# The end of a SwiGLU block: parts of 3, 4 and 4 pairs, half of the residual joined by DMA, and the last norm's two factors in one instruction

## The chip, the cores and the metric

The kernel runs on one core of a Trainium2 chip. Its five engines run on their own queues, each in order: TensorE (PE, matmuls into PSUM banks), VectorE (DVE), ScalarE (ACT), GpSimd (POOL) and SyncE (SP, which issues most DMAs). The metric is the device time of one execution in microseconds; the median of three runs of the kernel before is 1082.09 us (1082.02 to 1082.15).

## The reference

One layer of an encoder block on x of 512 rows and 1024 columns in float32, with the mixers left out here:

```python
x = x + merged @ w_o[l]
h2 = rmsnorm(x, g_ffn[l])
x = x + (jax.nn.silu(h2 @ w_ff_gate[l]) * (h2 @ w_ff_up[l])) @ w_ff_down[l]
return rmsnorm(x, g_final)

def rmsnorm(x, g):
    y = xf * lax.rsqrt(jnp.mean(xf * xf, axis=-1, keepdims=True) + EPS)
    return y * g
```

The hidden width of the SwiGLU is 2816, which is 11 pairs of 256 columns.

## The kernel before, in words

Every float32 product is made of three matmuls: each operand is split into a high part (a cast on ScalarE, L166) and a low part (a subtraction on VectorE, L167), and high x high, high x low and low x high are summed in a bank.

The SwiGLU's products are computed in a Strassen-like form with seven products in place of eight. The activations enter as a11, a12, s1, s2, s3, a22, s4 (quarters of the matrix and their sums), and the weights as seven forms: b11, b21, t1, t2, t3, t4, b22. The t forms are sums of weight quarters that VectorE adds in place (L239) ahead of the split. Up and gate projections go pair by pair: `pair(q)` (L817) makes products with matmuls of 256 columns (L730) and ends in `gated`, which multiplies the two branches (L752, L753), forms the sums for the next product (L769) and splits them into the activation tiles.

The 11 pairs are cut into parts by `FF_PARTS`: 4, 4 and 3 pairs. After each part comes the product with w_ff_down for the pairs of that part, with matmuls of 512 columns (L870 in `prod_tm`), n pairs giving 6 n matmuls for each of the seven forms. After the first two parts, `down` (L878) adds its results into `ydr`, a copy of x in DRAM, with DMAs from GpSimd that accumulate (L876). `x` was written there earlier, after the mixers.

The last part's product is written out from L912 on, and is the place of the change. Six banks hold the results: `a` (two, rows of the first or second half), `b` (two), `d` (two). a11 goes into `a`; a12 into `b`; s1 into `d`; s2 is added onto `a`; s3 onto that; a22 onto that; s4 onto `d`. So `a` has to be read out after a11, after s2 and after s3, before the next of them may write it. In the kernel before, two loads (L914) bring all of x from `ydr` into the tiles `y[0]` and `y[1]` (left and right 512 columns), and VectorE joins every bank with them: `to_y` (L946) adds, L960 and L964 subtract.

The final norm: `square` (L923) sums the squares of one block of 128 rows and one half on ScalarE and multiplies that half by the gain `gf` on VectorE (L924). `early` (L930) takes the half that is complete first, `store` the other: L936 gives the mean of squares, GpSimd raises it to -0.5 (L938), ScalarE scales the left half (L939), VectorE the right (L940), and two DMAs store them (L942). a22 and s4 are the two last products. Each is computed for one block of rows after the other, and `ev_a` or `ev_d` is called after each block, so the four blocks end one after the other.

Weights come in 128 x 1024 tiles through a pool of ten; the split halves `whi` and `wlo` come from pools of five, so a cast waits until the matmuls of the fifth piece before it are done. `PLAN` lists all weight pieces in order, and `take` prepares two ahead (`AHEAD`). The order of instructions on each engine is set when the kernel is built, by a scheduler that may move instructions past one another; within an engine nothing overtakes at run time.

Of the kernel before, what the change touches and what calls it, by code (L numbers as in the profile page):

```python
# [27 lines left out]
EPS = 1e-6  # L28
# [8 lines left out]
QH = CH // 2  # L37
NQ = NFB // 2

FF_PARTS = ((0, 4), (4, 4), (8, 3))  # L40

WARM = 8

# [5 lines left out]
def plan():  # L49
# [89 lines left out]
def block_kernel(ctx: ExitStack, tc: tile.TileContext, xT, xtok, wpack, wquad, cols, decs, rot, g_ffn, g_final, out):  # L139
    nc = tc.nc  # L140
# [5 lines left out]
    small = ctx.enter_context(tc.tile_pool(name="small", bufs=4))  # L146
# [202 lines left out]
    mhalf = const.tile([P, 8], F32, name="mhalf")  # L349
# [49 lines left out]
    for k in range(8):  # L399
# [16 lines left out]
                            op0=ALU.mult, op1=ALU.add)  # L416
    for j in range(15, 0, -2):
# [3 lines left out]
                                   op0=ALU.mult, op1=ALU.mult)  # L421
# [57 lines left out]
    def do_scores(h, qk):  # L479
        tab = decay(h)  # L480
        p = (bigtile(F32R), bigtile(F32R))
        for mb in range(NB):
            ps = bank()
            for d in range(2):
                sl = slice(mb * P, (mb + 1) * P)
                mm3(ps, (qk[0][:, 2 + d, sl], qk[1][:, 2 + d, sl]), (qk[0][:, d, :], qk[1][:, d, :]),
                    d == 0, d == 1)
            t = t512()
            o = (3 - mb) * P
            nc.vector.scalar_tensor_tensor(out=t, in0=ps, scalar=QK ** -0.5, in1=tab[:, o:o + 512],  # L490
                                           op0=ALU.mult, op1=ALU.mult)
            split(t, p[0][:, mb, :], p[1][:, mb, :])
        return p
# [101 lines left out]
    for h in range(HEADS):  # L595
        p = do_scores(h, qk)
# [47 lines left out]
    y = [bigtile(), bigtile()]  # L644
# [6 lines left out]
    ydr = dram.tile([S, D], F32, name="ydr")  # L651
# [48 lines left out]
    for half in range(2):  # L700
        c = Chunk()
# [15 lines left out]

    part_of = {q: (q0, n) for q0, n in FF_PARTS for q in range(q0, q0 + n)}
    act = {}
# [184 lines left out]
    begin(1, 1)  # L904
    for q0, n in FF_PARTS:
        for q in range(max(q0, 1), q0 + n):
# [10 lines left out]
    acs = [small.tile([P, 6], F32, tag="fin", name="fin") for _ in range(NB)]  # L917

    def square(nb, half):

        yt, ac = y[half][:, nb, :], acs[nb]
        sq = t512()
        nc.scalar.activation(sq, yt, AF.Square, accum_out=ac[:, half:half + 1])  # L923
        nc.vector.tensor_tensor(out=yt, in0=yt, in1=gf[:, half * 512:(half + 1) * 512], op=ALU.mult)  # L924

    def early(nb, half):

        square(nb, half)
        ac = acs[nb]
        nc.vector.tensor_scalar(out=ac[:, 3:4], in0=ac[:, half:half + 1], scalar1=1.0 / D, scalar2=EPS,  # L930
                                op0=ALU.mult, op1=ALU.add)

    def store(nb, half):
        square(nb, half)
        ac = acs[nb]
        nc.vector.scalar_tensor_tensor(out=ac[:, 4:5], in0=ac[:, half:half + 1], scalar=1.0 / D,  # L936
                                       in1=ac[:, 3:4], op0=ALU.mult, op1=ALU.add)
        nc.gpsimd.tensor_tensor(out=ac[:, 5:6], in0=ac[:, 4:5], in1=mhalf[:, 0:1], op=ALU.pow)  # L938
        nc.scalar.activation(y[0][:, nb, :], y[0][:, nb, :], AF.Copy, scale=ac[:, 5:6])  # L939
        nc.vector.tensor_scalar_mul(y[1][:, nb, :], y[1][:, nb, :], ac[:, 5:6])  # L940
        for h in (1, 0):
            nc.sync.dma_start(out[nb * P:(nb + 1) * P, h * 512:(h + 1) * 512], y[h][:, nb, :])  # L942

    def to_y(ps, nb, half):
        yt = y[half][:, nb, :]
        nc.vector.tensor_tensor(out=yt, in0=ps, in1=yt, op=ALU.add)  # L946

    a, b, d = ([bank(), bank()] for _ in range(3))
    prod_tm(n, "a11", a, True)
    for tt in range(2):  # L950
        to_y(a[tt], tt, 0)
    prod_tm(n, "a12", b, True, True)
    for tt in range(2):
        to_y(b[tt], tt, 0)
        early(tt, 0)
    prod_tm(n, "s1", d, True)
    prod_tm(n, "s2", a, False)
    for tt in range(2):
        yt = y[1][:, tt, :]
        nc.vector.tensor_tensor(out=yt, in0=yt, in1=a[tt], op=ALU.subtract)  # L960
    prod_tm(n, "s3", a, False)
    for tt in range(2):
        yt = y[1][:, 2 + tt, :]
        nc.vector.tensor_tensor(out=yt, in0=yt, in1=a[tt], op=ALU.subtract)  # L964
        to_y(d[tt], 2 + tt, 1)
        early(2 + tt, 1)

    def ev_a(tt):
        to_y(a[tt], 2 + tt, 0)
        store(2 + tt, 0)  # L970
# [69 lines left out]
```

## Time and profile before

| what | us |
|---|---|
| median of three runs | 1082.09 |
| the profiled execution | 1081.23 |
| its span, first to last instruction | 1079.4 |
| from the end of the last pair's s4 to the end of the last matmul | 30.12 |
| TensorE busy in it | 28.02 |
| from the last matmul's end to the end of the span | 10.29 |

A row of the timeline gives the start, the duration, the engine, the line in the kernel, the operation and the tiles (written <- read), and in brackets how long the engine was idle before it and who ended that. The rows of grouped instructions give the count, busy time in us and the mean duration in ns, and the idle time ahead. A row of the waits gives who waited for whom, the total, the count and the longest, in us. The profiled TensorE clock was 0.997 of full speed.

### The profile page before, as it was taken

How to read it: one execution, taken by the hardware profiler on the slowest of the kernel's cores; microseconds unless marked ns; L12 is line 12 of the kernel's file. 1: busy time of each engine (PE TensorE's matmuls, PEld its weight loads, DVE VectorE, ACT ScalarE, POOL GpSimd, SP SyncE). 2: the span in 40 equal slices, each digit the busy share in tenths (PEclk: the TensorE clock that was granted, in tenths of full speed). 3: DMA queues.
4: the chain of work that ended last, by engine and by line, in shares of the span. 5: the costliest groups of instructions: out<-in, count | busy, mean ns of one | idle time of the engine just before them, and what ended most of it. 6: DMA issues, size and time to landing. Idle time of an engine off the chain costs nothing. (4 is left out here: it accounts for less than half of the span.)

```text
span 1079.4 us, 13769 instructions
## 1 busy us (share of the span) xinstructions
PE 1062.5 (98%) x5560; PEld 913.8 (85%) x5560; DVE 743.5 (69%) x1012; ACT 429.8 (40%) x569; POOL 34.1 (3%) x50
## 2 busy tenths in 40 slices
PE   8999999999999999999999999999999999999995
PEld 7888888888888888888888888889998899989974
DVE  7846574757575746955364444459898979897997
ACT  7352244225222522222132323345555545554544
POOL 0000000000000000000000000000000100011001
PEclk9999999999999999999999999999999999999998
DMA  7322222212221322042323232922331942256402
GB/s 264 130 95 88 68 94 83 78 59 98 79 78 59 118 82 94 22 135 89 106 97 99 95 101 93 355 98 60 100 115 33 243 118 97 79 158 145 166 1 78
DMA packets 35727, 114.69 MB, mean 106 GB/s; under 512 B 4048, under 2 KB 4048, under 8 KB 35664
## 3 DMA queue, kind: packets, MB, share of 16 engines
q1 hardware_dynamic: 33360, 109.62, 30.4%
q0 software_dynamic: 2304, 4.20, 2.7%
q8 instruction: 43, 0.70, 0.3%
q14 instruction: 20, 0.16, 0.0%
HBM read 105.41 MB, written 8.39 MB: 105 GB/s over the span
## 5 line engine op out<-in xcount | busy, mean ns | idle before, releaser
L166 ACT CAST whi<-raw 128x1024 fp32r<-128x1024 f32 (+1 forms) x236 | 241.1, 1029 | 405.6 <-PE bank L281 136.8
L167 DVE TENSOR_TENSOR wlo<-raw,whi 128x1024 fp32r<-128x1024 f32 (+1 forms) x236 | 280.6, 1196 | 171.4 <-ACT whi L166 170.4
L281 PE MATMUL bank<-big,whi 128*128 128x512 f32 x640 | 249.0, 389 | 0.0
L280 PE MATMUL bank<-big,whi 128*128 128x512 f32 x640 | 249.0, 389 | 0.0
L282 PE MATMUL bank<-big,wlo 128*128 128x512 f32 x640 | 249.0, 389 | 0.0
L730 PE MATMUL bank<-xform,whi 128*128 128x256 f32 x1248 | 227.9, 284 | 1.2 <-ACT t L826 1.2
L730 PEld LDWEIGHTS bank<-xform,whi 128*128 128x128 f32 x1248 | 194.8, 192 | 4.4 <-ACT t L826 2.4
L730 PE MATMUL bank<-xform,wlo 128*128 128x256 f32 x624 | 175.6, 283 | 0.0
L281 PEld LDWEIGHTS bank<-big,whi 128*128 128x128 f32 x640 | 120.1, 188 | 25.0
L280 PEld LDWEIGHTS bank<-big,whi 128*128 128x128 f32 x640 | 120.1, 188 | 25.0
L282 PEld LDWEIGHTS bank<-big,wlo 128*128 128x128 f32 x640 | 120.1, 188 | 24.9
L280 PE MATMUL bank<-whi,big 128*128 128x512 f32 x304 | 118.3, 391 | 1.9 <-ACT big L169 1.6
L730 PEld LDWEIGHTS bank<-xform,wlo 128*128 128x128 f32 x624 | 119.4, 192 | 0.0
L281 PE MATMUL bank<-wlo,big 128*128 128x512 f32 x304 | 118.4, 389 | 0.4 <-DVE wlo L167 0.4
L282 PE MATMUL bank<-whi,big 128*128 128x512 f32 x304 | 118.2, 389 | 0.0
L870 PE MATMUL bank<-whi,big 128*128 128x512 f32 x308 | 96.3, 392 | 1.5 <-DVE big L960 0.9
L166 ACT CAST big<-t 128x512 fp32r<-128x512 f32 (+1 forms) x92 | 53.7, 593 | 99.8 <-DVE t L475 28.6
L239 DVE TENSOR_TENSOR raw<-raw 128x1024 f32<-128x1024 f32 x64 | 75.0, 1184 | 0.4
L870 PEld LDWEIGHTS bank<-whi,big 128*128 128x128 f32 x308 | 57.7, 188 | 15.3 <-ACT whi L166 1.4
L280 PEld LDWEIGHTS bank<-whi,big 128*128 128x128 f32 x304 | 57.0, 188 | 14.3 <-ACT big L169 1.9
L281 PEld LDWEIGHTS bank<-wlo,big 128*128 128x128 f32 x304 | 57.1, 188 | 12.6 <-DVE wlo L167 0.9
L282 PEld LDWEIGHTS bank<-whi,big 128*128 128x128 f32 x304 | 57.1, 188 | 11.9
(145 smaller groups left out, 919.5 us busy)
## 6 DMA issues: line engine op xcount, KB each, us to landing
raw<-wpack SPq DMA_DIRECT2D x118, 512.0 KB, 3.7
raw<-wquad SPq DMA_DIRECT2D x64, 512.0 KB, 4.3
ydr<-t POOLq DMA_DIRECT2D x16, 256.0 KB, 5.7
big<-xtok SPq DMA_DIRECT2D x2, 1024.0 KB, 6.3
ydr<-big SPq DMA_DIRECT2D x8, 256.0 KB, 2.1
big<-ydr SPq DMA_DIRECT2D x2, 1024.0 KB, 4.9
y<-big SPq DMA_DIRECT2D x8, 256.0 KB, 2.3
raw<-wpack SPq DMA_DIRECT2D x4, 256.0 KB, 6.0
```

Source lines behind the costliest of these rows:

```text
L166: nc.scalar.copy(hi, src)
L167: nc.vector.tensor_tensor(out=lo, in0=src, in1=hi.bitcast(F32), op=ALU.subtract)
L239: nc.vector.tensor_tensor(out=t, in0=t, in1=raws[quad, more, u][:, 0:n], op=ALU.add)
L280: nc.tensor.matmul(ps, lh, rh, start=first, stop=False)
L281: nc.tensor.matmul(ps, lh, rl, start=False, stop=False)
L282: nc.tensor.matmul(ps, ll, rh, start=False, stop=last)
L730: nc.tensor.matmul(o, l[:, c], r[:, k], start=start and s == 0 and k == 0 and i == 0, stop=stop and k == 3 and i == 2, skip_group_check=True)
L870: nc.tensor.matmul(pss[tt], l[:, k, sl], r[:, c], start=start and k == 0 and i == 0, stop=stop and k == n - 1 and i == 2, skip_group_check ...
```

## The change

`FF_PARTS` becomes 3, 4 and 4 pairs, so the last product has four. x of rows 256 to 511 is loaded into `y` as before, by two DMAs of half the size. For rows 0 to 255, `snap_y` copies the bank into `y` on ScalarE (L927), with sign -1 for s2, and a GpSimd DMA (L928) then adds x from `ydr` into that tile in SBUF. This replaces two `to_y` after a11 and the two subtractions after s2 on VectorE. b's two sums move behind s3's work in the code. In the norm, the separate multiplication by the gain goes, except for rows 128 to 255 in the left half (`gain`, L947); `store` scales and multiplies by the gain in one VectorE instruction (L955), and only the last block's left half is scaled by ScalarE (L953). The right half is stored as soon as it is scaled.

```diff
-FF_PARTS = ((0, 4), (4, 4), (8, 3))
+FF_PARTS = ((0, 3), (3, 4), (7, 4))
...
-    for half in range(2):
-        nc.sync.dma_start(y[half], ydr[:, half * 512:(half + 1) * 512].rearrange("(n p) c -> p n c", p=P))
+    for half in (1, 0):
+        nc.sync.dma_start(y[half][:, 2:4, :], ydr[2 * P:, half * 512:(half + 1) * 512].rearrange("(n p) c -> p n c", p=P))
...
-    def square(nb, half):
-        yt, ac = y[half][:, nb, :], acs[nb]
-        sq = t512()
-        nc.scalar.activation(sq, yt, AF.Square, accum_out=ac[:, half:half + 1])
-        nc.vector.tensor_tensor(out=yt, in0=yt, in1=gf[:, half * 512:(half + 1) * 512], op=ALU.mult)
...
+    def snap_y(ps, nb, half, sign):
+        yt = y[half][:, nb, :]
+        nc.scalar.activation(yt, ps, AF.Copy, scale=sign)
+        nc.gpsimd.dma_start(out=yt, in_=rows(nb, half), accum_op=ALU.add)
+    def to_y(ps, nb, half, last=False):
+        yt, ac, i = y[half][:, nb, :], acs[nb], sums[nb]
+        nc.vector.tensor_tensor(out=yt, in0=ps, in1=yt, op=ALU.add)
+        sq = t512()
+        nc.scalar.activation(sq, yt, AF.Square, accum_out=ac[:, i:i + 1])
+        if not last:
+            nc.vector.tensor_scalar(out=ac[:, 4:5], in0=ac[:, 0:1], scalar1=1.0 / D, scalar2=EPS,
+                                    op0=ALU.mult, op1=ALU.add)
+        else:
+            nc.vector.scalar_tensor_tensor(out=ac[:, 5:6], in0=ac[:, 1:2], scalar=1.0 / D,
+                                           in1=ac[:, 4:5], op0=ALU.mult, op1=ALU.add)
+            nc.gpsimd.tensor_tensor(out=ac[:, 7:8], in0=ac[:, 5:6], in1=mhalf[:, 0:1], op=ALU.pow)
+        sums[nb] += 1
+    def gain(nb, half):
+        yt = y[half][:, nb, :]
         nc.vector.tensor_tensor(out=yt, in0=yt, in1=gf[:, half * 512:(half + 1) * 512], op=ALU.mult)
...
-        nc.scalar.activation(y[0][:, nb, :], y[0][:, nb, :], AF.Copy, scale=ac[:, 5:6])
-        nc.vector.tensor_scalar_mul(y[1][:, nb, :], y[1][:, nb, :], ac[:, 5:6])
+    def store(nb, scaled=()):
+        for half in (1, 0):
+            yt = y[half][:, nb, :]
+            if half in scaled:
+                nc.scalar.activation(yt, yt, AF.Copy, scale=acs[nb][:, 7:8])
+            else:
+                nc.vector.scalar_tensor_tensor(out=yt, in0=yt, scalar=acs[nb][:, 7:8],
+                                               in1=gf[:, half * 512:(half + 1) * 512],
+                                               op0=ALU.mult, op1=ALU.mult)
+            nc.sync.dma_start(out[nb * P:(nb + 1) * P, half * 512:(half + 1) * 512], yt)
...
     prod_tm(n, "a11", a, True)
     for tt in range(2):
-        to_y(a[tt], tt, 0)
+        snap_y(a[tt], tt, 0, 1.0)
     prod_tm(n, "a12", b, True, True)
-    for tt in range(2):
-        to_y(b[tt], tt, 0)
-        early(tt, 0)
     prod_tm(n, "s1", d, True)
     prod_tm(n, "s2", a, False)
     for tt in range(2):
-        yt = y[1][:, tt, :]
-        nc.vector.tensor_tensor(out=yt, in0=yt, in1=a[tt], op=ALU.subtract)
+        snap_y(a[tt], tt, 1, -1.0)
     prod_tm(n, "s3", a, False)
     for tt in range(2):
         yt = y[1][:, 2 + tt, :]
         nc.vector.tensor_tensor(out=yt, in0=yt, in1=a[tt], op=ALU.subtract)
         to_y(d[tt], 2 + tt, 1)
-        early(2 + tt, 1)
+    for tt in range(2):
+        to_y(b[tt], tt, 0)
+    gain(1, 0)
...
     def ev_d(tt):
-        to_y(d[tt], tt, 1)
-        store(tt, 1)
+        to_y(d[tt], tt, 1, last=True)
+        store(tt, (0,) if tt else ())
```

How the instructions stand, at three places. First VectorE from the work around s2's end to s1's sums, before; banks 8473 and 8474 are `a`, 8477 and 8478 are `d`, `wlo` are the low parts of t3, t4 and b22.

```order
L167 TENSOR_TENSOR wlo_8579<-raw_8382,whi_8578 128x1024
L167 TENSOR_TENSOR wlo_8596<-raw_8417,whi_8595 128x512
L960 TENSOR_TENSOR big_8464<-big_8464,bank_8473 128x512
L960 TENSOR_TENSOR big_8464<-big_8464,bank_8474 128x512
L167 TENSOR_TENSOR wlo_8609<-raw_8237,whi_8608 128x1024
L239 TENSOR_TENSOR raw_8285<-raw_8285,raw_8349 128x512
L167 TENSOR_TENSOR wlo_8626<-raw_8285,whi_8625 128x512
L964 TENSOR_TENSOR big_8464<-big_8464,bank_8473 128x512
L964 TENSOR_TENSOR big_8464<-big_8464,bank_8474 128x512
L946 TENSOR_TENSOR big_8464<-bank_8477,big_8464 128x512
L946 TENSOR_TENSOR big_8464<-bank_8478,big_8464 128x512
```

The same place now; banks 8431 and 8432 are `a`, 8433 and 8434 `b`, 8435 and 8436 `d`; the `wlo` are those of t4 (8585, 8602) and of b22 (8637, 8641).

```order
L239 TENSOR_TENSOR raw_8195<-raw_8195,raw_8274 128x1024
L239 TENSOR_TENSOR raw_8243<-raw_8243,raw_8307 128x1024
L933 TENSOR_TENSOR big_8421<-bank_8433,big_8421 128x512
L167 TENSOR_TENSOR wlo_8585<-raw_8195,whi_8584 128x1024
L933 TENSOR_TENSOR big_8421<-bank_8434,big_8421 128x512
L167 TENSOR_TENSOR wlo_8602<-raw_8243,whi_8601 128x1024
L167 TENSOR_TENSOR wlo_8637<-raw_8437,whi_8636 128x1024
L167 TENSOR_TENSOR wlo_8641<-raw_8455,whi_8640 128x1024
L972 TENSOR_TENSOR big_8422<-big_8422,bank_8431 128x512
L972 TENSOR_TENSOR big_8422<-big_8422,bank_8432 128x512
L933 TENSOR_TENSOR big_8422<-bank_8435,big_8422 128x512
```

The subtractions after s2 (L960) are gone from VectorE, b's two sums stand among t4's splits, and both splits of b22 now stand ahead of the subtractions after s3 (L972).

Second, ScalarE in the same stretch, before: casts of t4 (8608, 8625) and b22 (8647, 8651), then squares.

```order
L166 CAST whi_8608<-raw_8237 128x1024
L166 CAST whi_8625<-raw_8285 128x512
L166 CAST whi_8647<-raw_8479 128x1024
L166 CAST whi_8651<-raw_8497 128x512
L923 ACTIVATE t512_8637,fin_8471<-big_8464 128x512
```

ScalarE now: casts of t4 (8584, 8601) and of b22 (8636, 8640).

```order
L166 CAST whi_8584<-raw_8195 128x1024
L166 CAST whi_8601<-raw_8243 128x1024
L927 ACTIVATE big_8422<-bank_8431 128x512
L927 ACTIVATE big_8422<-bank_8432 128x512
L166 CAST whi_8636<-raw_8437 128x1024
L166 CAST whi_8640<-raw_8455 128x1024
L935 ACTIVATE t512_8619,fin_8429<-big_8422 128x512
```

The two copies of s2's banks stand behind t4's casts and ahead of b22's.

Third, VectorE at the end of the program, before; `fin` tiles are one per block of rows (8471 and 8472 for rows 256 to 511, 8469 and 8470 for rows 0 to 255), banks 8478 and 8477 are those of s4.

```order
L936 SCALAR_TENSOR_TENSOR fin_8471<-fin_8471 128x1
L924 TENSOR_TENSOR big_8463<-big_8463,gf_8467 128x512
L940 TENSOR_SCALAR big_8464<-big_8464,fin_8471 128x512
L936 SCALAR_TENSOR_TENSOR fin_8472<-fin_8472 128x1
L924 TENSOR_TENSOR big_8464<-big_8464,gf_8467 128x512
L940 TENSOR_SCALAR big_8464<-big_8464,fin_8472 128x512
L936 SCALAR_TENSOR_TENSOR fin_8469<-fin_8469 128x1
L946 TENSOR_TENSOR big_8464<-bank_8478,big_8464 128x512
L940 TENSOR_SCALAR big_8464<-big_8464,fin_8469 128x512
L924 TENSOR_TENSOR big_8464<-big_8464,gf_8467 128x512
L936 SCALAR_TENSOR_TENSOR fin_8470<-fin_8470 128x1
L940 TENSOR_SCALAR big_8464<-big_8464,fin_8470 128x512
```

VectorE at the end now; `fin` 8430 is rows 384 to 511, 8427 and 8428 are rows 0 to 255.

```order
L933 TENSOR_TENSOR big_8421<-bank_8432,big_8421 128x512
L940 SCALAR_TENSOR_TENSOR fin_8430<-fin_8430 128x1
L955 SCALAR_TENSOR_TENSOR big_8422<-big_8422,fin_8430,gf_8425 128x512
L955 SCALAR_TENSOR_TENSOR big_8421<-big_8421,fin_8430,gf_8425 128x512
L933 TENSOR_TENSOR big_8422<-bank_8435,big_8422 128x512
L940 SCALAR_TENSOR_TENSOR fin_8427<-fin_8427 128x1
L933 TENSOR_TENSOR big_8422<-bank_8436,big_8422 128x512
L955 SCALAR_TENSOR_TENSOR big_8422<-big_8422,fin_8427,gf_8425 128x512
L955 SCALAR_TENSOR_TENSOR big_8421<-big_8421,fin_8427,gf_8425 128x512
L940 SCALAR_TENSOR_TENSOR fin_8428<-fin_8428 128x1
L955 SCALAR_TENSOR_TENSOR big_8422<-big_8422,fin_8428,gf_8425 128x512
```

Each block's power is still followed at once by an instruction that needs it, but two of them on VectorE in place of one, and the gains between are gone.

More of the change, by code (lines that the diff above doesn't have):

```diff
@@ L933, in store @@
[L933 to L942, printed above, removed]
@@ L944, in to_y @@
[L944 to L946 removed]
+    acs = [small.tile([P, 8], F32, tag="fin", name="fin") for _ in range(NB)]
+    sums = [0] * NB
+    def snap_y(ps, nb, half, sign):
[5 more added lines that the diff above has]
+        nc.vector.tensor_tensor(out=yt, in0=ps, in1=yt, op=ALU.add)
+        sq = t512()
+        nc.scalar.activation(sq, yt, AF.Square, accum_out=ac[:, i:i + 1])
[7 more added lines that the diff above has]
+        sums[nb] += 1
```

12 lines of the change are left out of this document (4 added, 8 removed).

## The prediction

> **What bounds the kernel now.** I read the page's first part, then stretches of the trace, then TensorE's waits, and last the end in order of time.
>
> ```profile
> span 1079.4 us, 13769 instructions
> PE 1062.5 (98%) x5560; PEld 913.8 (85%) x5560; DVE 743.5 (69%) x1012; ACT 429.8 (40%) x569; POOL 34.1 (3%) x50
> ```
>
> TensorE is busy for 98%, so only its idle time and the end after its last matmul can move. The next view gives busy time by stretch: the last product, the end behind it, and the second product, the one with four pairs that the table of parts leaves as it is.
>
> ```profile
> core 0: us, PE busy (x) PEld busy (x) DVE busy (x) ACT busy (x) POOL busy (x), PEclk, DMA share, GB/s
> 1039.02:1069.14 30.12, 28.02 (x119) 21.39 (x117) 28.65 (x47) 14.30 (x27) 0.50 (x1) 1.00 0.00 1
> 1069.14:1079.43 10.29, 0.00 (x0) 0.00 (x0) 4.04 (x10) 3.50 (x6) 2.33 (x4) 0.71 0.54 204
> 941.60:981.00 39.40, 39.40 (x179) 32.51 (x178) 36.97 (x41) 20.90 (x26) 5.44 (x7) 1.00 0.64 151
> ```
>
> The last product loses 2.10 us (30.12 - 28.02) with VectorE busy for 95% of it; the second, with VectorE at 94%, loses nothing. Behind the last matmul stand 10.29 us. TensorE's waits from 640 us on are all in the last pair and the last product:
>
> ```profile
> PE bank L730 <- ACT t L826: 1.2, 1, 1.2
> PE bank L870 <- DVE big L960: 0.9, 1, 0.9
> PE bank L870 <- DVE wlo L167: 0.6, 1, 0.6
> PE bank L870 <- ACT whi L166: 0.4, 1, 0.4
> PE bank L870 <- DVE big L964: 0.2, 1, 0.2
> ```
>
> The four on L870 are the 2.10 us. L960 and the L167 behind it are late because VectorE's queue is full. TensorE's pace and the end:
>
> ```profile
> 1061.00 0.40 PE L870 MATMUL bank<-wlo,big 128*128 128x512 f32 x1
> 1067.13 0.69 DVE L946 TENSOR_TENSOR big<-bank,big 128x512 f32<-128x512 f32 x1 [0.45 <-PE bank L870]
> 1068.41 0.68 DVE L924 TENSOR_TENSOR big<-big,gf 128x512 f32<-128x512 f32 x1
> 1068.64 0.88 POOL L938 TENSOR_TENSOR fin<-fin,mhalf 128x1 f32<-128x1 f32 x1 [86.10 <-DVE fin L936]
> 1068.75 0.39 PE L870 MATMUL bank<-whi,big 128*128 128x512 f32 x1
> 1069.55 0.49 DVE L940 TENSOR_SCALAR big<-big,fin 128x512 f32<-128x512 f32 x1 [0.46 <-POOL fin L938]
> 1070.03 0.68 DVE L924 TENSOR_TENSOR big<-big,gf 128x512 f32<-128x512 f32 x1
> 1070.25 0.86 POOL L938 TENSOR_TENSOR fin<-fin,mhalf 128x1 f32<-128x1 f32 x1 [0.73 <-DVE fin L936]
> 1071.62 0.68 DVE L946 TENSOR_TENSOR big<-bank,big 128x512 f32<-128x512 f32 x1
> 1071.78 0.54 POOL L938 TENSOR_TENSOR fin<-fin,mhalf 128x1 f32<-128x1 f32 x1 [0.67 <-DVE fin L936]
> 1074.56 0.54 POOL L938 TENSOR_TENSOR fin<-fin,mhalf 128x1 f32<-128x1 f32 x1 [2.24 <-DVE fin L936]
> 1075.14 0.72 ACT L939 ACTIVATE big<-big,fin 128x512 f32<-128x512 f32 x1 [1.45 <-POOL fin L938]
> ```
>
> From the second matmul of a22 (1061.00) to the last of s4 (1068.75) are 34 steps: 0.228 us each. The last matmul ends at 1069.14, but its sum L946 starts at 1071.62, 2.48 us late behind the blocks ahead of it in VectorE's queue; the last scale ends at 1075.86, 6.72 us behind TensorE.
>
> **The change part by part.** Durations that the terms use, by group:
>
> ```profile
> L946 DVE TENSOR_TENSOR big<-bank,big 128x512 f32<-128x512 f32 x10 | 6.6, 685 | 0.4 <-PE bank L870 0.4
> L167 DVE TENSOR_TENSOR wlo<-raw,whi 128x1024 fp32r<-128x1024 f32 x7 | 8.5, 1219 | 0.0
> L166 ACT CAST whi<-raw 128x1024 fp32r<-128x1024 f32 x6 | 6.3, 1049 | 4.0 <-issue 3.1 <-PE bank L730 0.5 <-DVE raw L239 0.3
> L923 ACT ACTIVATE t<-big 128x512 f32<-128x512 f32 x8 | 5.0, 625 | 7.2 <-DVE big L946 5.8 <-issue 1.4
> L938 POOL TENSOR_TENSOR fin<-fin,mhalf 128x1 f32<-128x1 f32 x4 | 2.8, 705 | 89.7 <-DVE fin L936 89.7
> L940 DVE TENSOR_SCALAR big<-big,fin 128x512 f32<-128x512 f32 x4 | 1.9, 486 | 1.6 <-POOL fin L938 1.6
> L677 DVE SCALAR_TENSOR_TENSOR t<-big,ac,gb 128x512 f32<-128x512 f32 x8 | 5.7, 748 | 2.4 <-POOL ac L673 2.4
> L769 DVE TENSOR_TENSOR t<-t,t 128x256 f32<-128x256 f32 x3 | 1.2, 415 | 0.0
> L848 ACT COPY t<-bank 128x512 f32<-128x512 f32 x8 | 4.5, 585 | 4.0 <-PE bank L870 4.0
> ```
>
> *The last product.* TensorE's work is moved, not changed: 24 matmuls a form instead of 18, 5.47 us instead of 4.10, and the weights grow alike. Ahead of a22's sums, VectorE loses eight instructions of 0.69 us (two sums of a11, two L960, four gains L924; its rows overlap by 0.08 us, so 4.9 us of queue). I walked the queues with these rows less the overlap, t = 0 at the end of the last pair's s4. VectorE starts on that pair's L841 at 0.4 (the longer cast and split ahead of it) and has ten instructions of 1024 columns (1.13 us), five of 512 (0.60) and four of 256 (0.34) ahead of b's first sum: 15.7, so it stands at 16.1. Two sums and two splits later a22's weights are done at 19.6; s4's cast, behind s2's copies on ScalarE, ends at 21.3, so VectorE has 1.8 us of slack where its queue was behind. s2 must leave its banks before s3: ScalarE's copy of the first half (0.59) can begin 1.37 us before s3 does, and the walk has it done at 19.0 against 19.7. That is costed at nothing; a 1.05 us cast just ahead of it would bring back 0.4. One stop stays: the split of s4's last weights waits for a buffer that s3's first 12 matmuls free (2.73 us), takes cast and split (1.05 + 1.22), and L972 (0.69) stands behind it: 5.8 us after s3's start, against 5.47. Each stop costs its idle time and 0.16 more, since rows last 0.39 us but follow at 0.228: now 2.10 + 4 x 0.16 = 2.74, then about 0.4. Term: **-2.3**, bounds -2.7 (no stop) and -1.2 (half of the stops stay).
>
> The last pair's results must also arrive in time. The second product shows how long they take, from s4's end (about 942.9) on:
>
> ```profile
> 942.96 0.68 DVE L841 TENSOR_TENSOR t<-bank,t 128x512 f32<-128x512 f32 x1
> 945.40 0.62 ACT L166 CAST big<-t 128x512 fp32r<-128x512 f32 x1 [2.51 <-DVE t L753]
> 946.42 0.68 DVE L167 TENSOR_TENSOR big<-t,big 128x512 fp32r<-128x512 f32 x1
> ```
>
> High part 3.1 us, low part 4.2 us. The last product asks for them after 17 and 22 matmuls (3.9 and 5.0 us): nothing. The first product, now of three pairs, asks after 12 and 15 (2.7 and 3.4): up to 0.8 lost by these rows, but its splits ahead are of half size, and the walk has both just in time. Term: **+0.3**, bounds 0 and +0.8.
>
> *The copy that the last pair waits for.*
>
> ```profile
> 1026.82 0.62 ACT L166 CAST whi<-raw 128x512 fp32r<-128x512 f32 x1 [1.02 <-issue]
> ...
> 1028.49 0.50 PE L730 MATMUL bank<-xform,whi 128*128 128x256 f32 x2 [1.17 <-ACT t L826]
> ```
>
> The cast ahead of L826 splits a11's second piece of weights; it grows from 512 to 1024 columns, 0.62 to 1.05, and TensorE has one more matmul (0.23) to fill with: +0.2, and I take **+0.3** (bounds +0.2 and +0.4), as that matmul also needs a low part from VectorE.
>
> *x by DMA.* ScalarE gains four copies (4 x 0.59 beside 14.30 us of 30.12; nothing), GpSimd four DMAs ahead of the powers in its queue, SP's loads of y shrink to half and stay ahead of the last weight loads. The trace has no DMA that adds into SBUF; the nearest are the sixteen that add into DRAM:
>
> ```profile
> DMA to landing us min/median/max: 3.6/5.7/9.3
> ```
>
> TensorE completes a11 after 24 matmuls of t = 0 (5.5), ScalarE's copy ends at 6.1, and the first DMA is issued at 6.2, so at the longest it lands at 15.5; b's sum, which waits for it with a22's splits behind it, stands at 16.1. The second pair has over 10 us. I take nothing, with +0.5 as the upper end.
>
> *The end.* Its chain starts where a22's first half ends; 36 matmuls (8.2 us) are then left, and four blocks of 128 rows follow. One block: sum 0.69; square, accumulator, small op and power up to the scale, by the rows above from 1067.82 to 1069.55, 1.73 with a power of 0.88, so 1.56 with the mean 0.705; two scale-and-gain instructions, 0.748 (L677) and 0.68 more with the overlap. VectorE is in order, so nothing runs under the power of rows 256-511. First block, with 0.3 for four squares that ScalarE has ahead: 0.69 + 1.56 + 0.3 + 1.43 = 3.98. Second and third: 0.61 + 1.56 + 1.43 = 3.6 each; the fourth sum lies under the third power, and then come small op, power and one scale, 0.28 + 0.705 + 0.748 = 1.73. Sum 12.9, 4.7 us behind TensorE, against 6.72 now: -2.0. The last stores:
>
> ```profile
> 1075.65 0.33 SPq L942 DMA_DIRECT2D y<-big  x1
> 1076.09 0.38 SPq L942 DMA_DIRECT2D y<-big  x1
> ```
>
> Now half 1 is issued before the last scale ends and half 0 0.23 us after its end; then both scales end together and the second issue follows 0.49 us after: +0.25. Term: **-1.75**. Bounds: powers of 0.88 (+0.7) and no overlap (+0.3) give -0.75; powers of 0.54 (-0.66) give -2.4.
>
> Here a rule bears on a row. The powers that began while an L924 ran took 0.88 and 0.86 us; the one beside L946 and the one beside nothing took 0.54. The Trainium skill, "SBUF — State Buffer", section "Who interferes with whom", says that a VectorE instruction with two SBUF inputs blocks a GpSimd instruction that reads SBUF until it has finished; L924 has two, L946 one and a bank, so the trace agrees. In the new order each scale waits for its power and no such instruction runs beside one, so by that rule all four take 0.54: the end would be -2.4 and the time 0.66 us less, 1077.9.
>
> *Sum.* -2.3 + 0.3 + 0.3 - 1.75 = -3.5 us. The profiled execution took 1081.23 us (span 1079.4 and 1.8 around it), so 1077.7 there; the median shown, 1082.09, lies 0.86 higher: **1078.6**.
>
> **The rivals.** About 0.2%, 2.2 us, can be told from no change.
>
> - *The end gives nothing.* VectorE now scales both halves of all but one block: 7 x 0.748 against 4 x 0.486, with powers that nothing covers. If late squares and handovers use up the 2.0 us, the end stays at 6.7: -2.3 + 0.6 + 0.25 = -1.5, 1080.6. For it: the in-order queue. Against: the 2.48 us that the last sum is late now.
> - *The stops stay.* VectorE is at 94% in the second product too, and splits of 1024 columns are lumpier. Then -1.75 + 0.6, 1080.9. Against: the second product's 39.40 of 39.40.
> - *Slower: the joined DMA lands late.* b's sum holds VectorE with a22's splits behind it; these end at 19.6 for use at 25.1, the first at 17.8, so 7.3 us more are covered, and from 6.2 + 17.2 on TensorE loses one for one. It loses the whole gain at 20.7 us from issue to landing; at 24, the time is 1085.4. Against: 9.3 is the longest of sixteen, and this stretch has a DMA share of 0.00.
>
> **How the numbers follow.** Forecast 0.66, with the power at either price; the end gives nothing 0.12; the stops stay 0.12; late DMA 0.04; a stop that I don't see, such as the first product's, 0.06. Faster 0.67, within 0.2% 0.22, slower 0.11 (late DMA, most of the unseen stop, a mix of the two middle cases). The terms' best ends (-2.7 + 0 + 0.2 - 2.4 = -4.9) give 1077.2; their worst (-1.2 + 0.8 + 0.4 + 0.5 - 0.75 = -0.25) give 1081.8. I take 1077.1 to 1081.6, which covers both middle rivals.
>
> **What would show it.** Right: TensorE's waits on L870 in the last product fall to one of about 0.3 us behind L972; the wait on L826 is 1.3 to 1.5 us; the four powers are at 0.54 to 0.7; the last scale ends 4 to 5.5 us behind the last matmul; no VectorE wait on the four DMAs. Wrong: waits on L167 or L166 in the first or last product, L933 waiting for a DMA, or an end of 6 us and more.

## The result, and the profile after

| | before | after |
|---|---|---|
| median of six runs each, us | 1082.12 | 1078.30 |
| lowest and highest | 1080.27 to 1082.86 | 1077.81 to 1079.21 |
| the profiled execution | 1081.23 | 1078.37 |
| its span | 1079.4 | 1076.3 |

The ratio of the times is 0.9967, with a 95% interval of 0.9954 to 0.998: the change makes the kernel about 3.6 us faster. In the later comparisons, of 10 to 15 runs each, the kernel before has medians of 1081.49 to 1081.63; in the one that measures the kernel after again, it is faster by 2.65 us (1081.49 against 1078.84).

The head of the page of the kernel after:

```profile
span 1076.3 us, 13768 instructions
PE 1062.6 (99%) x5560; PEld 914.0 (85%) x5560; DVE 739.8 (69%) x1004; ACT 430.8 (40%) x570; POOL 37.0 (3%) x54
```

TensorE's work is what it was (1062.6 against 1062.5), so all of the gain is idle time. TensorE's waits from the first product on, which were five, are two:

```profile
PE bank L870 <- DVE wlo L167: 1.4, 1, 1.4
PE bank L870 <- DVE big L972: 0.3, 1, 0.3
```

The first is the old wait on L826 under another name (below); the second is the one stop that VectorE still causes in the last product. The stretches, with the columns of the prediction's view: the last product to its last matmul's end, the end behind it, and the second product.

```profile
1030.87:1067.87 37.00, 36.63 (x160) 29.33 (x158) 30.90 (x45) 18.39 (x31) 4.61 (x6) 1.00 0.23 47
1067.87:1076.26 8.39, 0.00 (x0) 0.00 (x0) 3.01 (x6) 2.17 (x5) 1.08 (x2) 0.64 0.45 168
912.41:950.70 38.29, 38.29 (x170) 31.44 (x169) 35.88 (x39) 20.17 (x25) 5.20 (x6) 1.00 0.61 148
```

The last product's idle time fell from 2.10 to 0.37 us, with VectorE busy for 84% of it (30.90 of 37.00) where it had 95%; the end fell from 10.29 to 8.39. Two executions must be set side by side at the right place: the work ahead of the SwiGLU's pairs is unchanged, but takes up to 2.2 us more or less from one execution to the next. The same matmul in the profile of before, of after, and of a second profile of the kernel after:

```profile
736.77 0.48 PE L730 MATMUL bank<-xform,whi 128*128 128x256 f32 x2
```

```profile
736.86 0.36 PE L730 MATMUL bank<-xform,whi 128*128 128x256 f32 x1
```

```profile
738.98 0.48 PE L730 MATMUL bank<-xform,whi 128*128 128x256 f32 x2
```

From this matmul to the end of the span it is 342.67 us before, 339.40 after, and 339.25 in the second profile after (span 1078.2). This length, called the tail below, repeats to 0.15 us in these two profiles of one kernel (every other kernel has one), where medians have an interval of about 1.4 us to either side; so the experiments are compared by it. The 3.27 us between before and after consist of these, each product's loss taken as its time between first and last matmul less 0.2275 us (the pace of undisturbed matmuls) for each step:

| place | before | after | difference |
|---|---|---|---|
| loss in the last product | 3.34 | 0.89 | -2.45 |
| loss in the first product | 0.03 | 0.71 | +0.68 |
| the last pair, around L826 | | | +0.23 |
| the other pairs (gaps between short products) | 3.10 | 3.27 | +0.17 |
| from the last matmul's end to the last scale's end | 6.72 | 4.59 | -2.13 |
| from there to the end of the span | 3.58 | 3.80 | +0.22 |

Of the 0.89 us, 0.60 are the stop behind L972 (0.33 idle, 0.16 of overlap with the row before, 0.11 on the matmul behind). Another 0.31 go where a weight load waits for the high part of the last pair's result:

```profile
1034.28 0.62 ACT L166 CAST big<-t 128x512 fp32r<-128x512 f32 x1 [0.97 <-DVE t L753]
1034.95 0.19 PEld L870 LDWEIGHTS bank<-whi,big 128*128 128x128 f32 x1 [0.46 <-ACT big L166]
```

The end in order of time, in the kernel after: the fourth sum, the last two powers, and the last two scales, which run side by side.

```profile
1067.48 0.39 PE L870 MATMUL bank<-whi,big 128*128 128x512 f32 x1
1068.70 0.69 DVE L933 TENSOR_TENSOR big<-bank,big 128x512 f32<-128x512 f32 x1
1068.93 0.54 POOL L942 TENSOR_TENSOR fin<-fin,mhalf 128x1 f32<-128x1 f32 x1 [3.15 <-DVE fin L940]
1071.13 0.54 POOL L942 TENSOR_TENSOR fin<-fin,mhalf 128x1 f32<-128x1 f32 x1 [1.66 <-DVE fin L940]
1071.70 0.72 ACT L953 ACTIVATE big<-big,fin 128x512 f32<-128x512 f32 x1 [1.55 <-POOL fin L942]
1071.71 0.75 DVE L955 SCALAR_TENSOR_TENSOR big<-big,fin,gf 128x512 f32<-128x512 f32 x1 [0.72 <-POOL fin L942]
```

The last matmul ends at 1067.87, its sum begins 0.83 us later (2.48 before), and the last scale ends at 1072.46. As groups:

```profile
L955 DVE SCALAR_TENSOR_TENSOR big<-big,fin,gf 128x512 f32<-128x512 f32 x7 | 5.0, 749 | 2.3 <-POOL fin L942 2.2
L942 POOL TENSOR_TENSOR fin<-fin,mhalf 128x1 f32<-128x1 f32 x4 | 2.2, 545 | 16.8 <-DVE fin L940 16.8
L928 POOL DMA_DIRECT2D big<-ydr x4 | 3.5, 960 | 96.0 <-ACT big L927 96.0
```

All four powers are short. The four joining DMAs landed in time; no instruction waited for one:

```profile
DMA to landing us min/median/max: 3.8/4.6/6.1
```

### The profile page after: what moved, and what is told of

Same layout as the page of the kernel before. It is cut to its first block, busy times and chain, and to the rows that moved or that the text cites. A ratio compares the mean times of both kernels' runs of the same rounds, so it can differ in the third digit from the quotient of the medians.

```text
span 1076.3 us, 13768 instructions
## 1 busy us (share of the span) xinstructions
PE 1062.6 (99%) x5560; PEld 914.0 (85%) x5560; DVE 739.8 (69%) x1004; ACT 430.8 (40%) x570; POOL 37.0 (3%) x54
## 3 DMA queue, kind: packets, MB, share of 16 engines
q0 software_dynamic: 2880, 5.24, 3.3%
HBM read 105.41 MB, written 8.39 MB: 106 GB/s over the span
## 4 chain that ended last, share of the span: by engine, by line
PE 96%; DVE 2%; issue 1%; DMA 1%; ACT 0%; SPq 0%; POOL 0%; POOLq 0%; ACTq 0%; DVEq 0%
PE bank L281 22%; PE bank L282 22%; PE bank L280 22%; PE bank L730 21%; PE bank L870 9%; DMA big<-xT 1%; DVE big L955 0%; PE bank L692 0%; DVE wlo L167 0%; DVE sumsq L365 0%; ACT whi L166 0%; DVE big L933 0%; DVE big L170 0%; POOL fin L942 0%; ACT t L935 0%
```

## The experiments

The change has three parts: the cut into 3, 4, 4 pairs; the join of x by DMA in place of VectorE; and the norm with two factors at once. My theory: the parts take the stops out of the last product, the norm shortens the end, and the DMA join is worth little. The main rival: one of them alone does nearly all of it.

### The parts alone

The kernel before with the new cut:

```diff
-FF_PARTS = ((0, 4), (4, 4), (8, 3))
+FF_PARTS = ((0, 3), (3, 4), (7, 4))
```

> The kernel before with parts of 3, 4 and 4 pairs and nothing else. Theory (a larger last part gives VectorE's queue room by itself): the last product's loss against TensorE's pace falls from 3.3 us to about 1, the first product loses 0.7 and the copy in the last pair 0.3 as in the changed kernel, and the end shrinks by some 0.5 to 1: about -2, near 1080.2 us. Rival (only the sums taken off VectorE remove the stops): L960 and the splits are late as before, 2 us and more are lost, the end stays at 6.7 us, the first product still costs 0.7: no change or slightly slower, 1082 to 1083 us.

Measured: 1078.48 us, ratio 0.9968 (0.9956 to 0.998): nearly the whole gain, more than the theory allowed. The stretch from the last product's first matmul to its last scale's end, in this kernel and in the kernel before:

```profile
1031.19:1073.39 42.20, 36.86 (x160) 29.24 (x158) 37.27 (x59) 20.22 (x34) 2.50 (x4) 0.98 0.10 38
```

```profile
1039.02:1075.86 36.84, 28.02 (x119) 21.39 (x117) 32.69 (x57) 17.80 (x33) 2.82 (x4) 0.97 0.12 43
```

A fourth pair gives TensorE 41 matmuls more, 9.33 us, and VectorE only 4.58 us (37.27 - 32.69). VectorE's backlog at the end of the product is for the most part gone with the old norm and the old joins too: the loss fell to 1.23 us, and the last scale ended 4.87 us behind the last matmul instead of 6.72. I had costed that second fall to the norm.

### All but the parts

The kernel after with the old cut:

```diff
-FF_PARTS = ((0, 3), (3, 4), (7, 4))
+FF_PARTS = ((0, 4), (4, 4), (8, 3))
```

> The changed kernel with the old parts of 4, 4 and 3 pairs. Theory (the relief of VectorE is enough, the parts only cost): no loss of 0.7 in the first product, the copy in the last pair at 1.2, the stops of the last product at 0.4 to 0.8 in all, the end as in the changed kernel (4.6 us behind the last matmul): about 1077.5 us, 0.8 below the changed kernel. Rival (three pairs leave VectorE too little time): stops of 1.5 us and more return on L870, and the time is at or above the changed kernel's 1078.3.

Measured: 1077.80 us, ratio 0.9963 (0.9951 to 0.9976), near the theory's 1077.5, though the medians alone can't tell it from the kernel after. The tail is 338.77 us, 0.5 to 0.6 shorter than with the new cut. The stops are larger than the theory's 0.4 to 0.8: 0.9 us of waits, and a loss of 1.59 us in the last product, which is the rival's size. Its waits are the old one on L826 and two in the last product:

```profile
PE bank L730 <- ACT t L826: 1.2, 1, 1.2
PE bank L870 <- DVE big L972: 0.7, 1, 0.7
PE bank L870 <- ACT big L927: 0.2, 1, 0.2
```

### The join on VectorE, with either cut

First the kernel after with all of x loaded by SyncE, and the banks joined on VectorE; then the same with the old cut, so that only the norm is new.

```diff
...
-        nc.scalar.activation(yt, ps, AF.Copy, scale=sign)
-        nc.gpsimd.dma_start(out=yt, in_=rows(nb, half), accum_op=ALU.add)
+        nc.vector.tensor_tensor(out=yt, in0=yt, in1=ps, op=ALU.add if sign > 0 else ALU.subtract)
```

> The changed kernel with x for rows 0 to 255 joined on VectorE again (all of x loaded as before, a11 added and s2 subtracted by VectorE), all else kept. Four instructions of 0.6 us, 2.4 us, come back to VectorE's queue, which has 1.6 us of idle time before s4's splits and must let s2's bank go in time. Theory (the DMA is worth something only beyond that slack): 0.3 to 1.0 us slower than the changed kernel, 1078.6 to 1079.3, with the added wait of TensorE on the subtraction after s2. Rival 1 (the DMA carries most of the gain): 2 us slower and more, 1080.5. Rival 2: the slack hides all of it, no difference.

Measured: 1078.75 us, ratio 0.9968 (0.9956 to 0.9981), 0.45 above the kernel after and so within the theory's 0.3 to 1.0, though the tail, 339.55 us, puts it at 0.15 to 0.3 only. The wait on the subtraction after s2, which the theory expected, did not come: the last product lost even less, 0.26 us. But the last scale ended 5.52 us behind the last matmul instead of 4.59.

> Old parts of 4, 4, 3 pairs, all x joined on VectorE as before; of the change only the norm's two factors at once and the smaller number of gains are left. Theory, that both the accumulating DMAs and the dropped gains free VectorE in the last product, each for a part of it: the last product loses about 2.3 us against TensorE's pace (3.34 before, 1.59 with the DMAs as well), the last scale ends about 5.3 us behind the last matmul (6.72 before, 4.30 with the DMAs as well), time about 1079.3. Rival, that the dropped gains and the fused multiplication alone do it: loss 1.6, end 4.3 to 4.5, time about 1077.8. Second rival, that without the DMAs nothing of the stops goes: loss 3.3, time about 1080.4.

Measured: 1078.50 us, ratio 0.9971 (0.9962 to 0.998). The loss was 1.40 us, so without the DMAs the stops are even a little smaller (1.59 with them), as the first rival said of the stops (1.6); the end was 5.24 us, near the theory's 5.3, and the time lies between the two. What the DMAs free VectorE from comes back at the end of its queue, not at TensorE.

The same stretch as above, for the norm alone with the old cut, with the DMAs too, and for the new cut without and with the DMAs (the last is the kernel after):

```profile
1039.57:1072.98 33.41, 27.69 (x119) 21.46 (x117) 31.40 (x53) 15.74 (x30) 2.18 (x4) 0.98 0.13 47
```

```profile
1039.19:1071.86 32.67, 27.48 (x119) 21.53 (x117) 29.26 (x49) 17.62 (x34) 5.72 (x8) 0.97 0.33 81
```

```profile
1031.45:1073.34 41.89, 36.33 (x160) 29.39 (x158) 36.14 (x55) 18.57 (x31) 2.18 (x4) 1.00 0.10 38
```

```profile
1030.87:1072.46 41.59, 36.63 (x160) 29.33 (x158) 33.91 (x51) 20.56 (x35) 5.69 (x8) 0.97 0.26 63
```

From each length I take what TensorE needs at its pace, 26.78 us for three pairs and 36.11 for four (116 and 157 steps of 0.2275 and a last matmul of 0.39). What is left is all that the stretch loses, be it a stop or the end:

| us lost in the stretch | 4, 4, 3 | 3, 4, 4 |
|---|---|---|
| old norm, join on VectorE | 10.06 (before) | 6.09 |
| new norm, join on VectorE | 6.63 | 5.78 |
| new norm, join by DMA | 5.89 | 5.48 (after) |

The norm alone takes away 3.4, the cut alone 4.0, both 4.3: the two gains are for the most part the same one. The old norm with the DMA join was not run. That it is VectorE's queue which both relieve is read from its share of these stretches, 32.69 of 36.84 us before and 33.91 of 41.59 after, and was not tested apart. The DMA join adds 0.7 with the old cut and 0.3 with the new. The scheduler orders VectorE's end anew for each kernel, so a few tenths between two cells can also come from the order. The cut also costs some 1.1 us elsewhere (0.68 + 0.23 + 0.17 in the table of the result), so on top of the other two, where it brings 0.4 here, it loses 0.5 to 0.6. Medians can't tell this, tails do: 338.77 without the cut, 339.40 and 339.25 with it.

### What the first product loses, and why

Of the first product, three pairs instead of four, the prediction feared that the last pair's results come late. The trace has one gap of 0.09 us there. The others, 0.16 and 0.11 us at each of two places, lie at the handover of the banks behind s2 and behind s3. The rows around s2's end:

```profile
816.25 0.62 ACT L166 CAST whi<-raw 128x512 fp32r<-128x512 f32 x1 [0.38 <-PE bank L870]
816.88 1.26 ACT L848 COPY t<-bank 128x512 f32<-128x512 f32 x2
817.14 0.89 PE L870 MATMUL bank<-whi,big 128*128 128x512 f32 x2
```

Two matmuls in a row take 0.89 us there where others take 0.62: s3 wants the bank that L848 still copies, behind a cast. With an odd number of pairs the last piece of weights has one pair, so the two banks of a form are complete only three matmuls (0.68 us) apart; with four pairs it is six. First a kernel with the three pairs in the middle:

```diff
-FF_PARTS = ((0, 3), (3, 4), (7, 4))
+FF_PARTS = ((0, 4), (4, 3), (7, 4))
```

> The changed kernel with parts of 4, 3 and 4 pairs, so that the product of three pairs is the second. Theory (a product of three pairs asks for the last pair's results after 12 and 15 matmuls, wherever it stands): the second product loses about 0.7 us against TensorE's pace and the first less than 0.1; same time as the changed kernel within 0.3. Rival (the loss belongs to the first product's place): the loss goes, 0.6 us faster, 1077.7.

Measured: 1078.52 us, ratio 0.9968 (0.9956 to 0.9981). The first product now loses 0.03 us and the second 0.75, as expected: the loss belongs to the three pairs, wherever they are. Then a test of the cause: in a product of an odd number of pairs all matmuls for one bank come before those for the other, nine and nine.

```diff
-            if evict is None:
+            if evict is None and n % 2 == 0:
                 units = ((u, x),)
```

> The changed kernel, but in a product of three pairs both pieces of weights are used for one bank before the other bank's turn (nine matmuls, then nine, in place of six, six, three, three), so that 2.0 us instead of 0.7 lie between the ends of the two banks. Theory, that the first product's loss of 0.71 us comes from the short time for the copies of the two banks after s2 and s3: its loss falls to 0.1 or less, time about 0.6 less than the changed kernel, 1077.7. Rival, that the loss comes from weights split too late: it stays at 0.7 or grows, since the second piece is now needed 1.4 us earlier.

> The changed kernel as it is, beside the two others on the same chip: 1078.3, the first product losing 0.7 and the last 0.9 us.

Measured side by side: 1078.34 us (ratio 0.997, 0.9958 to 0.9981) against 1078.84 (0.9973, 0.9963 to 0.9983) for the kernel after. The first product of the kernel after, and of this one, each with the next four matmuls of the pairs:

```profile
800.90:830.40 29.50, 29.50 (x130) 23.55 (x129) 27.02 (x34) 18.28 (x25) 5.46 (x6) 1.00 0.66 182
```

```profile
801.69:830.60 28.91, 28.91 (x130) 23.70 (x129) 26.77 (x34) 17.64 (x25) 6.10 (x7) 1.00 0.68 184
```

The same 130 matmuls take 0.59 us less; the loss is 0.12. The tail is 338.63 us, 0.6 to 0.8 shorter. The theory holds: the price of three pairs was the handover of two banks, and the order of matmuls takes it away.

The same edit with the old cut, where the product of three pairs is the last one:

> Parts of 4, 4, 3 pairs with the rest of the change, and the same order of matmuls in products of three pairs, which here is the last one. Theory: the last product's loss of 1.59 us falls to 0.5 or less, since its stops lie at the handover of banks (0.11, 0.43 and 0.99 us in three places), time about 1.1 less than with 4, 4, 3 alone: 1076.7, faster than the changed kernel. Rival, that the stops belong to VectorE's backlog or to the weights: loss 1.5 or more, time 1077.8 or more.

Measured: 1077.93 us, ratio 0.9967 (0.9954 to 0.998). Here the theory is half right, and this half is instructive. TensorE's stops in the last product are gone, 0.10 us instead of 1.59, and it is done 1.8 us earlier, at 1065.76. But the last scale still ends at 1071.85, where it was 1071.86:

```profile
1038.88:1071.85 32.97, 26.88 (x119) 21.70 (x117) 29.32 (x49) 17.77 (x34) 5.67 (x8) 0.96 0.33 80
```

32.97 us, against 32.67 with the stops. What TensorE gained was lost again behind it, but VectorE's instructions do not stand there in the same order, so this is no test of the stops alone. With the stops, each sum (L933) from the second block on ran under the power of the block ahead. Now VectorE is ordered so:

```profile
1061.72 0.69 DVE L933 TENSOR_TENSOR big<-bank,big 128x512 f32<-128x512 f32 x1 [0.52 <-PE bank L870]
1062.99 0.37 DVE L940 SCALAR_TENSOR_TENSOR fin<-fin 128x1 f32<-128x1 f32 x2
1063.89 2.74 DVE L955 SCALAR_TENSOR_TENSOR big<-big,fin,gf 128x512 f32<-128x512 f32 x4 [0.53 <-POOL fin L942]
1066.54 1.28 DVE L933 TENSOR_TENSOR big<-bank,big 128x512 f32<-128x512 f32 x2
```

The first block's small op (L940) stands behind the second block's sum, which waits for TensorE, and both sums of s4 stand behind four scales, with no power to run under. Taking the stops away gained nothing in this kernel; what they cost with the order kept is not shown.

### More work off VectorE, by two more DMAs

If VectorE's own work sets that end, two subtractions less should shorten it. To the last kernel I added the DMA join for the right half of rows 256 to 511, in place of SyncE's load of that half:

```diff
...
-        yt = y[1][:, 2 + tt, :]
-        nc.vector.tensor_tensor(out=yt, in0=yt, in1=a[tt], op=ALU.subtract)
-        to_y(d[tt], 2 + tt, 1)
+        snap_y(a[tt], 2 + tt, 1, -1.0)
     for tt in range(2):
         to_y(b[tt], tt, 0)
+    for tt in range(2):
+        to_y(d[tt], 2 + tt, 1)
```

> Parts of 4, 4, 3 with the merged order of the last product, and x joined by an accumulating DMA in the right half of rows 256-511 too, so that VectorE does two subtractions of 0.68 us less in the last product, ScalarE two copies and GpSimd two DMAs more. Theory, that VectorE's own work sets the end there (29.2 us busy of the 33.0 from the product's first matmul to the last scale, while TensorE is done 6.1 us earlier): the stretch shrinks by 0.6 to 1.3 us, time about 1077.0. Rival, that the chain from the last matmul through square, power and scale sets it: the stretch stays at 33.0, time 1077.9. Second rival, that the two later DMAs land only after VectorE asks for them (landing 3.8 to 6.1 us so far): VectorE waits on a DMA, the stretch grows by 0.5 or more, time 1078.4 or more.

Measured: 1080.54 us, ratio 0.9988 (0.9978 to 0.9998): most of the gain is lost, by the second rival. The stretch, the rows of the last DMA and of the sums that wait, VectorE's waits, and the landings:

```profile
1039.18:1074.38 35.20, 27.34 (x119) 21.55 (x117) 28.17 (x47) 18.78 (x36) 7.42 (x10) 0.95 0.40 89
```

```profile
1057.96 0.69 DVE L167 TENSOR_TENSOR wlo<-raw,whi 128x512 fp32r<-128x512 f32 x1 [0.17 <-ACT whi L166]
1058.83 0.86 POOL L928 DMA_DIRECT2D big<-ydr  x1 [0.65 <-ACT big L927]
1061.89 1.29 DVE L933 TENSOR_TENSOR big<-bank,big 128x512 f32<-128x512 f32 x2 [3.23 <-DMA big<-ydr]
```

```profile
DVE big L933 <- DMA big<-ydr: 3.7, 2, 3.2
```

```profile
DMA to landing us min/median/max: 3.6/4.4/5.5
```

VectorE has 1.15 us less to do (28.17 against 29.32) and waits 3.7 us for DMAs that are no slower than the others; the stretch grew by 2.2. VectorE was done with all else at 1058.65, and the last DMA was issued at 1058.83. So the prediction's slower rival is real: it needs no slow DMA, only a reader that comes sooner behind the issue than the 3.6 to 5.5 us of a landing. That VectorE's work alone sets the end of three pairs is consistent with this sum, but it wasn't shown apart from the wait.

### What makes a power long

Before, two of four powers took 0.86 to 0.88 us. Two kernels add a multiplication on VectorE under each power of the kernel after; its operands are both in SBUF in the first, one of them in a bank of PSUM in the second.

```diff
             nc.gpsimd.tensor_tensor(out=ac[:, 7:8], in0=ac[:, 5:6], in1=mhalf[:, 0:1], op=ALU.pow)
+            nc.vector.tensor_tensor(out=sq, in0=sq, in1=gf[:, 0:512], op=ALU.mult)
```

```diff
+            nc.vector.tensor_tensor(out=sq, in0=ps, in1=sq, op=ALU.mult)
```

> The changed kernel with one more VectorE multiplication right behind the sum of squares of each of the last four blocks, two operands in SBUF, 128x512; its product is used nowhere. Theory, that the power on GpSimd takes 0.86 to 0.88 us instead of 0.54 when VectorE reads two operands from SBUF beside it: the powers under the added multiplications take about 0.88, and the last scale ends 1 to 1.4 us later behind the last matmul (4.59 in the changed kernel), since VectorE is also 0.7 us longer busy ahead of each block's scale; the span 1 to 1.4 longer. Rival, that the long powers of the kernel before had another cause: the powers stay at 0.54.

> The same added multiplication with one operand in SBUF and the other in a bank of PSUM; its product is used nowhere. Theory: the powers stay at 0.54 to 0.56, and what the end grows by is VectorE's own added time alone, 0.7 us or less. Rival, that any VectorE instruction beside the power lengthens it: 0.86 to 0.88 as with two operands.

Measured, one execution of each: 1079.39 and 1078.55 us. The groups of the first, then of the second:

```profile
L942 POOL TENSOR_TENSOR fin<-fin,mhalf 128x1 f32<-128x1 f32 x4 | 3.5, 864 | 16.8 <-DVE fin L940 16.8
L943 DVE TENSOR_TENSOR t<-t,gf 128x512 f32<-128x512 f32 x4 | 2.7, 684 | 0.0
```

```profile
L943 DVE TENSOR_TENSOR t<-bank,t 128x512 f32<-128x512 f32 x4 | 2.7, 683 | 0.0
L942 POOL TENSOR_TENSOR fin<-fin,mhalf 128x1 f32<-128x1 f32 x4 | 2.2, 545 | 16.8 <-DVE fin L940 16.8
```

VectorE's added work is the same to a nanosecond; only where its operand lies differs. The power takes 864 ns beside two operands in SBUF and 545 beside one. From the last product's first matmul to the last scale it is 42.84 us in the first kernel and 41.58 in the second, against 41.59 in the kernel after: the 1.26 us between the two match four powers at 0.32 more, one behind the other. VectorE's own 0.68 us fits under each power and costs nothing. The rule of the Trainium skill that the prediction weighed ("SBUF — State Buffer", section "Who interferes with whom") holds here, with these numbers.

### Another split of the last scales

The kernel after with the old cut, and the gain multiplied early for half of each of the last blocks, so that ScalarE can scale that half beside VectorE:

```diff
...
-    gain(1, 0)
+    for tt in range(2):
+        gain(2 + tt, 1)
+    for tt in range(2):
+        gain(tt, 0)
...
-        store(2 + tt)
+        store(2 + tt, (1,))
...
-        store(tt, (0,) if tt else ())
+        store(tt, (0,))
```

> The changed kernel with parts of 4, 4, 3 pairs, and the last scales shared out another way: the gain is multiplied in early for the right half of rows 256-511 and the left half of rows 0-255, ScalarE scales those halves and VectorE the others with the fused multiplication. Theory: the end falls only a little, because VectorE's sum of the fourth block stands behind the third block's scale: the last scale about 4.1 us behind the last matmul against 4.30, and the two added gains of rows 256-511 fit into VectorE's idle time, so time about 1077.5 against 1077.8. Rival, that the added gains bring a stop of the last product back: 1078.3 or more. Rival, that the end falls by a full scale on VectorE, 0.75: about 1077.0.

Measured: 1077.91 us, ratio 0.9965 (0.9953 to 0.9978), neither better nor worse than 1077.80. The loss stayed at 1.60, but the last scale ended 4.47 us behind the last matmul, not 4.1. The fourth block's square now stands behind the third block's scale in ScalarE's queue:

```profile
1069.48 0.72 ACT L953 ACTIVATE big<-big,fin 128x512 f32<-128x512 f32 x1 [0.82 <-POOL fin L942]
1070.11 0.61 ACT L935 ACTIVATE t<-big 128x512 f32<-128x512 f32 x1
```

Work taken from one queue stood in the way in another. By their tails the best kernels are the kernel after with merged odd products (338.63), all but the cut (338.77) and this one (338.86). By time none is distinguishable from the kernel after; all their intervals overlap.

## Why the prediction was right, step by step

- *The last product, -2.3 forecast:* -2.45. One stop of 0.3 us behind L972 stayed, as the walk of the queues had it. That the difference fits is in part luck, since both its ends were too low: 2.74 and 0.4 us of loss forecast, 3.34 and 0.89 measured. The last pair's results, which the prediction took for in time, account for 0.31 us of the 0.89: their high part came 3.87 us behind the pair's s4 (1031.03 to 1034.90), not 3.1. And the reason was too narrow. I treated the stops and the end as two terms with a cause each; the table of six kernels points to one queue, whose lateness appears as stops or as a late last scale. With three pairs 1.5 us of stops could be taken away with nothing gained, though there VectorE's order changed with them.
- *The first product, +0.3 forecast with a bound of 0.8:* +0.68. The size is within the bounds, the cause was missed. The last pair's results cost 0.1 at most; the copies of two banks only 0.68 us apart cost the rest. I had walked this handover in the last product, with its 1.37 us, and not in the product that has an odd number of pairs now.
- *The copy in the last pair, +0.3 forecast:* +0.23 for the stretch. I named the copy L826, with 1.3 to 1.5 us, as what TensorE would wait for. The trace names the filler matmul's low part:

```profile
1018.82 1.22 DVE L167 TENSOR_TENSOR wlo<-raw,whi 128x1024 fp32r<-128x1024 f32 x1
1019.68 0.58 ACT L826 COPY t<-bank 128x512 f32<-128x512 f32 x1
1020.09 0.50 PE L870 MATMUL bank<-wlo,big 128*128 128x512 f32 x1 [1.38 <-DVE wlo L167]
```

The low part ended at 1020.04 and the copy at 1020.26, so the two come within 0.22 us of each other; the added matmul's need of a low part, which the prediction mentioned, decides who is named.

- *x by DMA, 0 forecast:* no wait on a DMA, and landings of 3.8 to 6.1 us against an allowance of 9.3. But 0 was too little: against a join on VectorE the DMAs are worth 0.15 to 0.3 us in the tail here and 0.7 with the old cut, since they shorten VectorE's queue.
- *The end, -1.75 forecast:* -1.91 (-2.13 up to the last scale, 4.59 us behind the last matmul where 4.7 stood; +0.22 for the stores where +0.25 stood). Here errors cancelled, which is luck. The powers were all at 0.545, which the prediction's mean of 0.705 put 0.16 higher each; the added multiplications show why. With that price the prediction had -2.4. But its chain around the power was too short, because its 1.73 us (1067.82 to 1069.55 before) joins two blocks: the sum at 1067.13 waited for s4's first half, which ended 2.05 us ahead of the last matmul's end, while the power at 1068.64 is the first of the four and belongs to a22's first block, as the order of the `fin` tiles shows. In the kernel after one block's rows stand alone:

```profile
1063.46 0.68 DVE L933 TENSOR_TENSOR big<-bank,big 128x512 f32<-128x512 f32 x1
1065.24 0.54 POOL L942 TENSOR_TENSOR fin<-fin,mhalf 128x1 f32<-128x1 f32 x1 [3.15 <-DVE fin L940]
1065.82 1.42 DVE L955 SCALAR_TENSOR_TENSOR big<-big,fin,gf 128x512 f32<-128x512 f32 x2 [0.72 <-POOL fin L942]
```

From the sum's end (1064.14) to the scale it is 1.68 us, of which 1.14 are not the power, where the prediction had 0.85 (1.73 less a power of 0.88).

- *What was not foreseen:* +0.17 us in the gaps of the other pairs, about 0.1 in the second profile; its cause was not tried.
- *The rivals:* neither the end nor the stops stayed as they were. A late DMA did not happen here, and did happen once the join was moved to where its reader follows at once.

Terms summed to -3.5 us; the span from the same matmul on shrank by 3.27, and the profiled executions differ by 2.86, since the time around the span was 2.1 us after and 1.8 before. That the sum is within 0.2 is again partly luck: the first product and the other pairs lost 0.38 and 0.17 more than forecast, and the last product, the copy and the end 0.15, 0.07 and 0.16 less. The median came out 0.3 below the forecast.

## What to carry to other kernels

When two edits relieve the same in-order queue, cost them together: measured one at a time each can show nearly the whole gain, and their sum is no estimate. A stop of the busiest engine near the end is worth removing only if the queues behind it then end sooner, so look at the order in which the scheduler leaves them. Before cutting a loop into odd pieces, look at how long two banks' ends lie apart, and set that against the copies that must empty them.

## What the runs showed of the hardware

A power on GpSimd of 128 x 1 elements takes 545 ns on average alone or beside a VectorE multiplication with one operand in PSUM, and 864 ns beside one with both operands in SBUF, in all four powers of each kernel. An accumulating DMA of 256 KB into SBUF landed 3.6 to 6.1 us after its issue over ten instances in two kernels, each taking 0.86 to 1.24 us of GpSimd's own time to issue; so it is free for a sum 6.1 us away and costs that sum the difference when it is nearer. The stretch ahead of the SwiGLU's pairs, which none of these kernels changes, brought the same matmul near their start at 736.77 us in one profile and at 738.98 in another, while the tails of two profiles of the same kernel agreed to 0.15 us.
